# Transposing attention probabilities as float32r from tiles that a DMA fills

## The chip, the cores and the metric

The kernel runs on one core of a Trainium2 chip. The metric is the device time of one execution in microseconds. Below, PE is the matrix engine (TensorE), PEld its weight loads, DVE the vector engine, ACT the scalar engine, POOL the GpSimd engine, SP the engine that only issues DMAs.

## The reference

An encoder trunk of two layers on 512 tokens of width 1024. Layer 0 mixes tokens by gated linear attention, layer 1 by softmax attention, and each is followed by a gated MLP with a width-3 convolution. The change is in layer 1:

```python
def attn_mixer(h, w_qkv, q_norm, k_norm, w_out, cos, sin):
    ...                                  # q: 8 heads, k and v: 2, of 128; rmsnorm and rope on q and k
    scale = ATTN_HEAD_DIM ** -0.5
    def block(q_blk):                    # 128 queries of each head
        s = jnp.einsum('bkgqd,bksd->bkgqs', q_blk, k).astype(jnp.float32) * scale
        p = jax.nn.softmax(s, axis=-1).astype(v.dtype)
        return jnp.einsum('bkgqs,bksd->bkgqd', p, v)
    o = lax.map(block, qb)
    ...
    return o @ w_out
```

All of it is in float32.

## The kernel before

The activations `x` lie in SBUF as eight tiles of 128 features by 512 tokens. Nearly all matmuls are in float32r, a shorter form of float32: each operand is split into a high part, which is its float32r value, and a low part, the rest, and a product is three matmuls, high x high, high x low and low x high (`mm3`, lines 266 to 268; `out_steps`, line 323; `token_steps`, line 297). Weights arrive in tiles `raw` of 1 MB by SP's DMAs. `Weights.half` hands out one half after the other and makes the next one ready: either ACT and DVE split it (lines 143, 144), or, for the attention's query, key and value weights and part of the output's, ACT writes the high part and its negative and a DMA on POOL's queue adds `raw` to that (lines 123, 124, 133).

Attention runs over 32 blocks, 8 heads of 4 blocks with 128 queries each. For block t of the loop over `t`:

- `scores` (line 772): one `mm3` into a bank of the PSUM tag `s` (2 banks), then on DVE the row maximum `mx` (line 781) and the bias `nb` (782), then on ACT the exponential `p` (784), which also gives the row sums. A `p` is a float32 tile of 128 x 512 of the SBUF tag `t`, of which there are 6.
- `shares`: DVE inverts the sum (`rc`, 789) and scales `p` (790).
- `turn`: for the block LAG = 4 steps earlier, four transposes of 128 x 128 on PE into a bank of the tag `pt` (802), then ACT writes the high part `pth` (805) and DVE the low part `ptl` (806).
- `mix`: LAG2 = 6 steps behind, for every second block, twelve matmuls with the values into `po`.

Between them stand steps of other work, listed by `plan`: the projections of the query pairs 1 to 3 (`qpair`; `feature_steps` is the matmuls `A` and `B`, 48 instructions to a pair), placed by `Q_STEPS`, and what makes a pair ready (norm, rotation, splitting), placed by `Q_READY`. Each entry gives a first block and how many steps of the generator are taken at that block and the following ones. `O_STEPS` places twelve steps of the output projection `op`; the rest of it follows the loop. The recording layer that builds the program takes the order of the code as a priority and may move an instruction ahead of others; the order on each engine is fixed when the program is built.

A transpose of a float32 tile uses `ident`, a float32 identity. The same identity serves the linear attention (lines 489, 561) and the spreading of norms (line 207). The tag `sq` has 3 tiles: squares of `x` for the norms (lines 240, 244), squares of queries, and the router weights `rraw` of layer 0. The sums of squares go to PE as `ms` (line 252).

Of the kernel before, what the change touches and what calls it, by code (L numbers as in the profile page):

```python
# [8 lines left out]
F32 = mybir.dt.float32  # L9
F32R = mybir.dt.float32r  # L10
# [4 lines left out]
P = 128  # L15
S = 512
D = 1024
KC = D // P
# [10 lines left out]

GATE_STEPS, GATE_LAG = (1, 3, 5, 7, 10, 12, 15, 17), 2  # L30

LAGS = (4, 6)

Q_STEPS = {1: (0, (4,) * 4), 2: (4, (3, 3, 2, 2, 2, 2, 2)), 3: (11, (2,) * 8)}
Q_READY = {1: (4, (3, 3, 2, 1, 1, 0, 1)), 2: (11, (3, 2, 2, 1, 1, 1, 0, 1)), 3: (19, (3, 2, 2, 1, 1, 1, 0, 1))}

O_STEPS = (22, 23, 25, 27, 29, 31, 32, 33, 34, 35, 36, 37)


PC_NORM = 0  # L40
# [6 lines left out]
def hybrid_encoder_kernel(  # L47
# [20 lines left out]
    nc = tc.nc  # L68
    pe, act, dve, pool, sync = nc.tensor, nc.scalar, nc.vector, nc.gpsimd, nc.sync
    mm = pe.matmul  # L70

    cp = ctx.enter_context(tc.tile_pool(name="cp", bufs=1))
    sp = ctx.enter_context(tc.tile_pool(name="sp", bufs=1))
# [4 lines left out]
    def nm(s):  # L78
        uid[0] += 1
        return f"{s}{uid[0]}"  # L80
# [3 lines left out]
    def bank(tag, n):  # L84
        return pp.tile([P, S], F32, tag=tag, bufs=PS[tag], name=nm(n))
# [4 lines left out]
    def big(dt, n):  # L90
        return pair("g", 22, dt, n)

    def tmp(tag, n, w=S):
        return sp.tile([P, w], F32, tag=tag, bufs={"u": 4, "t": 6, "sq": 3}[tag], name=nm(n))

    def tiny(w, n, tag="tiny"):
        return sp.tile([P, 8], F32, tag=tag, bufs={"tiny": 36, "tiny2": 4}[tag], name=nm(n))[:, :w]
# [73 lines left out]
        sync.dma_start(raw[c // 4][:, r], w_vg[c // 4, :, r])  # L171
        W.raw[id(w_vg), c // 4] = raw[c // 4]

    ident = cp.tile([P, P], F32, name="ident")
    make_identity(nc, ident)

    two = tmp("u", "two")
    dve.memset(two[:, :P], 2.0 ** -5)
    dve.memset(two[:, P : 2 * P], -(2.0 ** -6))
# [30 lines left out]
    class Norm:  # L210
# [27 lines left out]
        def square(self, c):  # L238
            q = tmp("sq", "sq")
            act.activation(q, x[c], AF.Square)  # L240
            if self.ss is None:
                self.ss = q
            else:
                dve.tensor_tensor(self.ss, self.ss, q, ALU.add)
            self.done += 1
# [18 lines left out]
    def mm3(ps, wh, wl, mh, ml, start, stop):  # L264

        mm(ps, wh, mh, start=start, stop=False)  # L266
        mm(ps, wh, ml, start=False, stop=False)  # L267
        mm(ps, wl, mh, start=False, stop=stop)  # L268
# [74 lines left out]
    def gla(norm, nxt):  # L343
# [36 lines left out]
        cw = cp.tile([P, 2 * 2 * FC * 4], F32, name="cw")  # L380


        rraw = sp.tile([P, KC * 32], F32, tag="sq", bufs=3, name="rraw")
        sync.dma_start(rraw, w_r)
        rw = pair("wh", 3, F32R, "rw")
        rv = rraw.rearrange("p (k o c) -> p k o c", k=KC, o=1)
# [13 lines left out]
        norm.rows()  # L400

        rf = tmp("t", "rf")
        dve.tensor_tensor(rf, rp, norm.R, ALU.mult)
        rst = sp.tile([P, S], F32R, tag="t", bufs=6, name="rst")
        act.activation(rst, rf, AF.Copy)
        dve.tensor_tensor(rst[32:64, :], rf[32:64, :], rst[32:64, :].bitcast(F32), ALU.subtract)

# [228 lines left out]
    def attention(norm, nxt):  # L636
# [90 lines left out]
        def qpair(i, tag="acc"):  # L727
            head, sc = yield from roped(1 + i, PC_QK, float(HD), "qsc", tag)
            for e in range(2):
                y = head(e)  # L730
                yield
                t = big(F32R, "q")
                split(y, t)
                heads[2 * i + e] = (t, sc, e)
                yield
# [34 lines left out]
        probs, pts, pos = {}, {}, {}  # L770

        def scores(h, j):

            qt, sc, e = heads[h]
            kt = kk[h // 4]
            js = slice(j * P, (j + 1) * P)
            s = bank("s", "s")
            mm3(s, qt[:, js], qt[:, S + j * P : S + (j + 1) * P], kt[:, :S], kt[:, S:], True, True)
            scj = sc[:, 2 * j + e : 2 * j + e + 1]
            mx, nb, sm, rc = (tiny(1, n) for n in ("mx", "nb", "sm", "rc"))  # L780
            dve.reduce_max(mx, s, axis=mybir.AxisListType.X)
            dve.tensor_scalar(nb, mx, scj, -1.0, ALU.mult, ALU.mult)
            p = tmp("t", "p")
            act.activation(p, s, AF.Exp, scale=scj, bias=nb, accum_out=sm)
            probs[h, j] = (p, sm, rc)

        def shares(h, j):
            p, sm, rc = probs[h, j]
            dve.reciprocal(rc, sm)
            dve.tensor_scalar(p, p, rc, None, ALU.mult)  # L790
            probs[h, j] = p

        def turn(h, j):

            hf, i = divmod(j, 2)
            if i == 0:
                pts[h, hf] = tuple(big(F32R, n).rearrange("p (k q) -> p k q", q=256) for n in ("pth", "ptl"))
            ph3, pl3 = pts[h, hf]
            p = probs.pop((h, j))
            tp = bank("pt", "pt")  # L800
            for k in range(NT):
                pe.transpose(tp[:, k * P : (k + 1) * P], p[:, k * P : (k + 1) * P], ident)  # L802
            isl = slice(i * P, (i + 1) * P)
            tp3 = tp.rearrange("p (k q) -> p k q", q=P)
            act.activation(ph3[:, :, isl], tp3, AF.Copy)
            dve.tensor_tensor(pl3[:, :, isl], tp3, ph3[:, :, isl].bitcast(F32), ALU.subtract)

        def mix(h, hf):
            ph3, pl3 = pts.pop((h, hf))
            vo = (h // 4) * HD  # L810
            if hf == 0:
                pos[h] = bank("po", "po")
            dst = pos[h][:, hf * 256 : (hf + 1) * 256]
            for k in range(NT):
                vsl = slice(k * 256 + vo, k * 256 + vo + HD)
                mm3(dst, vh[:, vsl], vl[:, vsl], ph3[:, k, :], pl3[:, k, :], k == 0, k == NT - 1)
            if hf == 1:
                t = big(F32R, "oT") if h < 4 else pair("xhl", 8, F32R, "oT")
                split(pos[h], t)
                oh[h] = (t[:, :S], t[:, S:])  # L820

        LAG, LAG2 = LAGS
        blocks = [(h, j) for h in range(QH) for j in range(NT)]
        osteps = out_steps(w_aout, oh, nxt)
        plan = collections.defaultdict(list)
        for i in range(1, QH // 2):
            g = qpair(i)
            for first, counts in (Q_STEPS[i], Q_READY[i]):
                for t, n in enumerate(counts):
                    plan[first + t] += [g] * n  # L830
        for t in O_STEPS:
            plan[t].append(osteps)
        for t in range(len(blocks) + LAG2):
            if t < len(blocks):
                scores(*blocks[t])
            for g in plan[t]:
                next(g, None)
            if LAG <= t < len(blocks) + LAG:
                turn(*blocks[t - LAG])
            if t < len(blocks):  # L840
                shares(*blocks[t])
            if t >= LAG2:
                h, j = blocks[t - LAG2]
                if j % 2 == 1:
                    mix(h, j // 2)
        whole(osteps)

    norms = [Norm(i) for i in range(4)]
    cw = gla(norms[0], norms[1])
    ffn(0, norms[1], cw, norms[2])  # L850
    attention(norms[2], norms[3])
    ffn(1, norms[3], cw, None)

# [80 lines left out]
```

## Time and profile before

| | us |
|---|---|
| median of 3 runs (lowest, highest) | 1133.26 (1132.57, 1133.51) |
| the profiled execution, its own time | 1133.16 |
| its span | 1131.4 |
| PE busy, share of the span | 99% |
| DVE, ACT, POOL busy | 61%, 43%, 7% |
| first scores to last transposes of the attention | 625.4 to 734.2 |

The granted clock of PE is 1.00 over the run. A row of the profile names the line of the kernel, the engine, the operation, the tile that is written and those that are read. Matmuls overlap in their records, so their durations add up to more than their time; what one costs is the distance between the starts of two in a row. In the chain of work that ended last each step is followed back to what released it.

### The profile page before, as it was taken

Reading aid. Unit: us, or ns where it says so; the run is one execution under the profiler, and the core shown is the slowest. Engines: PE = TensorE matmul, PEld = TensorE weight load, DVE = VectorE, ACT = ScalarE, POOL = GpSimd, SP = SyncE. Lnnn points to the kernel's source line nnn. Section 1 sums busy time; section 2 is a strip of 40 time slices with the busy share of each in tenths; the row PEclk is TensorE's granted clock in tenths of the full one; section 3 lists DMA queues with packets and bytes.
Section 4 is the critical chain, followed back from the end, with each engine's and each line's share of the span. In section 5 each row is a group of like instructions: output and inputs, shape, how many; then the busy total and the mean of one; then the engine's idle time right before and its main releaser. Section 6 shows DMA issues by size and latency. Waiting matters only on the chain.

```text
span 1131.4 us, 12991 instructions
## 1 busy us (share of the span) xinstructions
PE 1125.7 (99%) x5260; PEld 939.2 (83%) x5260; DVE 690.1 (61%) x996; ACT 482.1 (43%) x690; POOL 76.0 (7%) x66
## 2 busy tenths in 40 slices
PE   9999999999999999999999999999999999999998
PEld 7888888888888888888888888888888888888887
DVE  6787563677777777633325589766777777762221
ACT  5564232444444444422234667644444444442210
POOL 0104110000000000000004433000000000000000
PEclk9999999999999999999999999999999999999999
DMA  6422211232322323223247633223232232323320
GB/s 231 149 75 78 84 63 38 75 112 75 112 97 90 112 75 112 100 86 112 77 152 181 149 76 75 56 75 112 75 112 85 101 112 75 112 84 121 130 93 19
DMA packets 19980, 111.66 MB, mean 99 GB/s; under 512 B 2384, under 2 KB 3024, under 8 KB 8400
## 3 DMA queue, kind: packets, MB, share of 16 engines
q1 hardware_dynamic: 17328, 102.29, 25.9%
q0 software_dynamic: 2304, 8.39, 3.9%
q8 instruction: 41, 0.67, 0.2%
q10 hardware_dynamic: 288, 0.15, 0.0%
q14 instruction: 19, 0.16, 0.0%
HBM read 100.34 MB, written 2.10 MB: 91 GB/s over the span
## 4 chain that ended last, share of the span: by engine, by line
PE 99%; DVE 0%; DMA 0%; ACT 0%; issue 0%; SPq 0%; DVEq 0%; ACTq 0%
PE up L266 14%; PE up L267 14%; PE up L268 14%; PE vg L297 8%; PE op L323 8%; PE dn L266 7%; PE dn L268 7%; PE dn L267 7%; PE o L548 2%; PE pt L802 1%; PE av L297 1%; PE kv L524 1%; PE A L266 1%; PE A L268 1%; PE A L267 1%; PE B L266 1%
## 5 line engine op out<-in xcount | busy, mean ns | idle before, releaser
L143 ACT ACTIVATE wh<-raw 128x1024 fp32r<-128x1024 f32 x164 | 173.3, 1056 | 351.4 <-PE up L267 132.8
L144 DVE TENSOR_TENSOR wl<-raw,wh 128x1024 fp32r<-128x1024 f32 x164 | 203.7, 1242 | 144.8 <-ACT wh L143 144.6
L266 PE MATMUL up<-xhl,wh 128*128 128x512 f32 x704 | 274.3, 390 | 0.0
L268 PE MATMUL up<-xhl,wl 128*128 128x512 f32 x704 | 273.9, 389 | 0.0
L267 PE MATMUL up<-xhl,wh 128*128 128x512 f32 x704 | 273.9, 389 | 0.0
L268 PEld LDWEIGHTS up<-xhl,wl 128*128 128x128 f32 x704 | 132.2, 188 | 27.6
L266 PEld LDWEIGHTS up<-xhl,wh 128*128 128x128 f32 x704 | 132.2, 188 | 27.4
L267 PEld LDWEIGHTS up<-xhl,wh 128*128 128x128 f32 x704 | 132.2, 188 | 27.1
L266 PE MATMUL dn<-gu,wh 128*128 128x512 f32 x352 | 136.9, 389 | 0.0
L267 PE MATMUL dn<-gu,wh 128*128 128x512 f32 x352 | 136.9, 389 | 0.0
L268 PE MATMUL dn<-gu,wl 128*128 128x512 f32 x352 | 136.9, 389 | 0.0
L603 DVE TENSOR_TENSOR u<-up,R 128x512 f32<-128x512 f32 x88 | 60.3, 687 | 52.7 <-PE up L268 52.7
L297 PE MATMUL vg<-wh,xhl 128*128 128x512 f32 x256 | 79.7, 390 | 0.6 <-DVE halfneg L184 0.6
L605 ACT ACTIVATE y<-u,cw 128x512 f32<-128x512 f32 x88 | 71.2, 811 | 20.4 <-DVE u L603 20.4
L268 PEld LDWEIGHTS dn<-gu,wl 128*128 128x128 f32 x352 | 66.1, 188 | 13.8
L267 PEld LDWEIGHTS dn<-gu,wh 128*128 128x128 f32 x352 | 66.1, 188 | 13.7
L266 PEld LDWEIGHTS dn<-gu,wh 128*128 128x128 f32 x352 | 66.1, 188 | 13.6
L323 PE MATMUL op<-oT,wh 128*128 128x512 f32 x256 | 70.9, 395 | 0.0
L607 DVE SCALAR_TENSOR_TENSOR y<-u,cw,y 128x511 f32<-128x511 f32 x88 | 65.9, 751 | 2.9
L606 DVE SCALAR_TENSOR_TENSOR y<-u,cw,y 128x511 f32<-128x511 f32 x88 | 65.6, 746 | 0.6 <-ACT y L605 0.6
L609 ACT ACTIVATE y<-y 128x512 f32<-128x512 f32 x44 | 27.9, 634 | 87.8 <-DVE y L607 87.8
L297 PEld LDWEIGHTS vg<-wh,xhl 128*128 128x128 f32 x256 | 48.0, 188 | 10.6 <-ACT sq L240 0.7
(186 smaller groups left out, 1432.1 us busy)
## 6 DMA issues: line engine op xcount, KB each, us to landing
raw<-in_w_up_dram SPq DMA_DIRECT2D x44, 1024.0 KB, 4.8
raw<-in_w_down_dram SPq DMA_DIRECT2D x22, 1024.0 KB, 4.8
wl<-raw POOLq DMA_DIRECT2D x16, 512.0 KB, 4.7
raw<-in_w_vg_dram SPq DMA_DIRECT2D x6, 1024.0 KB, 4.7
raw<-in_w_akq_dram SPq DMA_DIRECT2D x5, 1024.0 KB, 5.2
raw<-in_w_kq_dram SPq DMA_DIRECT2D x4, 1024.0 KB, 4.8
raw<-in_w_gout_dram SPq DMA_DIRECT2D x4, 1024.0 KB, 4.8
raw<-in_w_aout_dram SPq DMA_DIRECT2D x4, 1024.0 KB, 4.9
```

The lines of the kernel that those rows point to most:

```text
L143: act.activation(hi[:, sl], r[:, sl], AF.Copy)
L144: dve.tensor_tensor(lo[:, sl], r[:, sl], hi[:, sl].bitcast(F32), ALU.subtract)
L266: mm(ps, wh, mh, start=start, stop=False)
L267: mm(ps, wh, ml, start=False, stop=False)
L268: mm(ps, wl, mh, start=False, stop=stop)
L297: mm(ps[j][:, :width], hl[k][i == 2][:, j * P : (j + 1) * P], (wl if i == 1 else wh)[:, sl], start=k == 0 and i == 0, stop=k == KC - 1 and ...
L323: mm(pss[ng][n], wt[:, sl], mv, start=k == 0 and i == 0, stop=k == KC - 1 and i == 2)
L603: dve.tensor_tensor(u, ps, norm.R, ALU.mult)
L605: act.activation(y, u, AF.Identity, scale=w(1), bias=w(3))
L606: dve.scalar_tensor_tensor(y[:, 1:], u[:, : S - 1], w(0), y[:, 1:], ALU.mult, ALU.add)
L607: dve.scalar_tensor_tensor(y[:, : S - 1], u[:, 1:], w(2), y[:, : S - 1], ALU.mult, ALU.add)
L609: act.activation(res[1], res[1], AF.Silu)
```

## The change

Probabilities are no longer transposed from the tile in which they were computed. One block later a DMA on ACT's queue copies them, bit for bit, into a tile declared float32r, and the transposes read that tile, with an identity declared float32r. The loop turns a block five steps after its scores and mixes it seven steps after. Probabilities and copies share the tag `t`, now of seven tiles; the squares get two tiles instead of three, the router weights move from the squares' tag to `t`, and the identity is first made in a temporary tile and then copied. The pairs' projections and their making ready are placed anew (pair 1 in three blocks instead of four, pairs 2 and 3 evenly in eight, all made ready in seven blocks, so that each pair is complete one block sooner), and so are the steps of the output projection. In the built order PE's instructions outside the attention are the same as before. In the changed kernel the copies are line 800, the transposes line 812, their evacuation lines 815 and 816, the scaling line 794 and the exponential line 788.

```diff
-LAGS = (4, 6)
-
-Q_STEPS = {1: (0, (4,) * 4), 2: (4, (3, 3, 2, 2, 2, 2, 2)), 3: (11, (2,) * 8)}
-Q_READY = {1: (4, (3, 3, 2, 1, 1, 0, 1)), 2: (11, (3, 2, 2, 1, 1, 1, 0, 1)), 3: (19, (3, 2, 2, 1, 1, 1, 0, 1))}
-
-O_STEPS = (22, 23, 25, 27, 29, 31, 32, 33, 34, 35, 36, 37)
+LAGS = (5, 7)
+
+Q_STEPS = {1: (0, (5, 5, 6)), 2: (3, (2,) * 8), 3: (11, (2,) * 8)}
+Q_READY = {i: (t, (3, 3, 2, 1, 1, 0, 1)) for i, t in ((1, 3), (2, 11), (3, 19))}
+
+O_STEPS = (22, 24, 26, 28, 30, 32, 33, 34, 35, 36, 37, 38)
...
-        return sp.tile([P, w], F32, tag=tag, bufs={"u": 4, "t": 6, "sq": 3}[tag], name=nm(n))
+        return sp.tile([P, w], F32, tag=tag, bufs={"u": 4, "t": 7, "sq": 2}[tag], name=nm(n))
...
-    ident = cp.tile([P, P], F32, name="ident")
-    make_identity(nc, ident)
+
+    eye = tmp("u", "eye")[:, :P]
+    make_identity(nc, eye)
+    identr = cp.tile([P, P], F32R, name="ident")
+    dve.tensor_copy(identr, eye)
+    ident = identr.bitcast(F32)
...
-        rraw = sp.tile([P, KC * 32], F32, tag="sq", bufs=3, name="rraw")
+        rraw = sp.tile([P, KC * 32], F32, tag="t", bufs=7, name="rraw")
...
-        rst = sp.tile([P, S], F32R, tag="t", bufs=6, name="rst")
+        rst = sp.tile([P, S], F32R, tag="t", bufs=7, name="rst")
...
+        def copy(h, j):
+
+            t = sp.tile([P, S], F32R, tag="t", bufs=7, name=nm("pr"))
+            act.dma_start(t.bitcast(F32), probs[h, j])
+            probs[h, j] = t
+
...
-                pe.transpose(tp[:, k * P : (k + 1) * P], p[:, k * P : (k + 1) * P], ident)
+                pe.transpose(tp[:, k * P : (k + 1) * P].bitcast(F32R), p[:, k * P : (k + 1) * P], identr)
...
         for t in range(len(blocks) + LAG2):
             if t < len(blocks):
                 scores(*blocks[t])
+            if 1 <= t <= len(blocks):
+                copy(*blocks[t - 1])
```

## The prediction

> **What bounds the kernel now.** I read the page first, for the engine that carries the span, then the transposes by their tile, then the neighbours of the same shape for what a faster transpose could cost, and last the waits and the timeline where the attention's engines meet.
>
> ```profile
> PE 1125.7 (99%) x5260; PEld 939.2 (83%) x5260; DVE 690.1 (61%) x996; ACT 482.1 (43%) x690; POOL 76.0 (7%) x66
> PE 99%; DVE 0%; DMA 0%; ACT 0%; issue 0%; SPq 0%; DVEq 0%; ACTq 0%
> ```
>
> The first line is busy time, the second the shares of the chain that ended last. TensorE (PE) is on that chain for 99% of the span of 1131.4 us. So time goes or comes only as PE time: a matmul that becomes shorter, or a gap that opens in PE's row. Nothing outside the attention changes PE's instructions; there the 128 transposes of the probabilities are what the change makes shorter.
>
> ```profile
> L802 PEld LDWEIGHTS pt<-ident,p x128: 137/139/227, 643.6 to 734.1; 128*128 128x128 f32 x128
> L802 PE MATMUL pt<-ident,p x128: 270/272/309, 643.8 to 734.2; 128*128 128x128 f32 x128
> ...
> 649.57 0.60 PE L802 MATMUL pt<-ident,p 128*128 128x128 f32 x4
> ...
> 121.96 1.95 PE L501 MATMUL in<-ek 128*128 128x128 f32 x16
> 234.21 0.95 PE L252 MATMUL ms<-ones,sq 128*128 128x1 f32 x8
> ...
> L501 PEld LDWEIGHTS in<-ek x64: 190/192/192, 121.8 to 175.7; 128*128 128x128 f32 x64
> L501 PE MATMUL in<-ek x64: 275/275/275, 122.0 to 175.8; 128*128 128x128 f32 x64
> ...
> L252 PE MATMUL ms<-ones,sq x32: 164/250/250, 27.3 to 773.3; 128*128 128x1 f32 x32
> ...
> 614.09 11.52 PE av L297 x96
> ...
> 740.11 27.23 PE op L323 x120
> ```
>
> Matmuls overlap in their records, so what one costs is its pace, start to start. Four transposes last 0.60 us and one 0.272, so the pace is (0.60 - 0.272) / 3 = 0.109 us, and 128 of them are 14.0 us of PE. The last two rows are pieces of the chain, of float32r matmuls only: 256 columns (av) at 11.52 / 96 = 0.120 us, 512 columns (op) at 27.23 / 120 = 0.227 us. That is 0.107 us for 256 columns more, and 0.013 us that each matmul costs beside its columns. The plain float32 matmuls "in" have 128 columns and yet a pace of (1.95 - 0.275) / 15 = 0.112 us.
>
> **The change, part by part.** *The transposes.* The same 128 instructions, now with float32r data and identity. If a float32r transpose streams its 128 columns once, the row of float32r matmuls gives 0.013 + 0.107 / 2 = 0.067 us. It then saves 0.109 - 0.067 = 0.042 us, times 128 = 5.4 us. Two things bound this. The weight load must keep up: an ordinary load ("in") is recorded at 192 ns and holds a pace of 0.100 to 0.112 us ("ms" has a single column to stream, so there is nothing but the load: (0.95 - 0.25) / 7 = 0.100); that of a transpose is 139 ns, 53 less, which leaves 0.047 to 0.059, under 0.067. If the 0.013 is not paid, the pace is that load's at most 0.059 and the saving 6.4 us. At the other end, with the load of an ordinary float32r matmul, nothing is saved (the first rival). I take 5.4, because the row for the load of a transpose is the nearest one.
>
> *The copies.* 32 DMAs of 256 KB, from SBUF to SBUF, issued on ACT's queue, each behind the exponential of the next block. The trace has no such DMA; the nearest are the stores of the output, of the same size, and the one that ACT issues at the end.
>
> ```profile
> out_dram<-x SPq DMA_DIRECT2D x7, 256.0 KB, 2.1
> ...
> 1128.61 0.36 ACTq L633 DMA_DIRECT2D out_dram<-x  x1
> ...
> DMA to landing us min/median/max: 1.7/2.0/4.6
> ...
> 630.00:645.00 15.00, 15.00 (x73) 12.32 (x73) 9.91 (x24) 9.67 (x17) 3.46 (x4) 1.00 0.83 200
> 690.00:705.00 15.00, 14.74 (x98) 12.75 (x97) 13.24 (x31) 10.68 (x22) 7.87 (x6) 1.00 0.19 36
> ```
>
> A copy holds ACT's sequencer for 0.36 us. What is queued behind it on ACT is the evacuation of the transposed block and then the next exponential. The window rows give PE, PEld, DVE, ACT and POOL busy: ACT, at its fullest, is busy 10.68 of 15 us, with 15 / 2.74 = 5.5 blocks in them (the step between the two exponentials quoted below); 5.5 x 0.36 = 2.0 us more still fits. At best the issue runs while the exponential before it executes (0.78 us) and costs nothing. A copy waits for the scaled probabilities; in DVE's queue these stand ahead of the next block's bias, for which the exponential ahead of the copy waits anyway, so ACT's queue gets no new wait from them. Copies are landed by the store row in 2.1 us, between 1.7 and 4.6.
>
> Whether this shows on PE is a matter of the distance from scaling to transpose. In the built order of the changed kernel the early transposes stand five blocks behind; in the last third they stand directly behind the scores of three or four blocks later, as they do now:
>
> ```profile
> 715.30 0.48 DVE L790 TENSOR_SCALAR p<-p,rc 128x512 f32<-128x512 f32 x1
> 717.97 0.48 DVE L790 TENSOR_SCALAR p<-p,rc 128x512 f32<-128x512 f32 x1
> ...
> 716.40 0.78 ACT L784 ACTIVATE p<-s,nb,qsc 128x512 f32<-128x512 f32 x1
> 719.14 0.77 ACT L784 ACTIVATE p<-s,nb,qsc 128x512 f32<-128x512 f32 x1
> ...
> 719.88 0.27 PE L802 MATMUL pt<-ident,p 128*128 128x128 f32 x1
> 721.66 0.60 PE L802 MATMUL pt<-ident,p 128*128 128x128 f32 x4
> ...
> PEld s L266 <- ACT p L784: 1.7, 4, 0.7
> PE s L266 <- ACT p L784: 0.3, 1, 0.3
> ```
>
> These are blocks 26 and 27: scaled by 715.78 and 718.45, transposed from 719.88 and 721.66. A copy issued at the next block's exponential (716.40, 719.14) and landed 2.1 us later is there at 718.5 and 721.24: 1.4 and 0.4 us ahead of the transpose. So at 2.1 us it is hidden, with little to spare. The bounds are 0 and the second rival's 8.4 us; I take 1.0 us, for the half of a dozen late blocks where 0.4 us or less is left. The last two rows are the waits that exist now, where scores wait for a bank that an exponential still reads: at most 2.0 us, and I leave them as they are, since PE's work per block in that third stays at about the 2.74 us between the exponentials (the op groups that moved make up for the shorter transposes). If they went, that would be 2.0 us more of gain.
>
> *Seven tiles.* Probabilities and copies share them. In the built order nearly every exponential waits for the landing of a copy issued two blocks earlier, over 5 us; one or two copies wait for the one issued a block earlier, about 3 us. Hidden at 2.1, and at 4.6 part of the second rival.
>
> *Pairs a block sooner.* The projection's matmuls are the same in number. The third pair's weights are needed sooner by one group of scores, 3 matmuls at op's 0.227 = 0.7 us of PE, while the first copies share the DMA engines (0.83 busy in the window row above).
>
> ```profile
> raw<-in_w_up_dram SPq DMA_DIRECT2D x44, 1024.0 KB, 4.8
> ...
> 629.57 0.89 POOL L133 DMA_DIRECT2D wl<-raw  x1
> 641.16 0.39 PE L268 MATMUL A<-xhl,wl 128*128 128x512 f32 x1
> DMA to landing us min/median/max: 5.0/5.4/9.1
> ```
>
> The load issued at 629.57 is the one of 9.1 us: landed by 638.7, used at 641.16, 2.5 us later. 0.7 less leaves 1.8; a copy ahead of it takes some quarter of a 1024 KB load's 4.8 us, 1.2 us. One is hidden, two cost 0.6. I put it at nothing, and the 0.6 into the range.
>
> *Two square buffers instead of three, the identity, the router's tile.* The square of the last chunk now waits for the addition of the one before.
>
> ```profile
> 769.68 0.62 ACT L240 ACTIVATE sq<-x 128x512 f32<-128x512 f32 x1
> ...
> 770.14 0.68 DVE L244 TENSOR_TENSOR sq<-sq,sq 128x512 f32<-128x512 f32 x1
> 771.41 0.68 DVE L244 TENSOR_TENSOR sq<-sq,sq 128x512 f32<-128x512 f32 x1
> 772.61 0.95 PE L252 MATMUL ms<-ones,sq 128*128 128x1 f32 x8
> ```
>
> 770.82 + 0.62 (a square) + 0.68 = 772.12 instead of 772.09, and PE asks at 772.61. The extra copy of the identity is a DVE instruction of under 1 us ahead of the first transposes. Nothing.
>
> *Sum.* The profiled execution took 1133.16 us (span 1131.4 and 1.8 around it); the median of the runs is 1133.26. 1133.2 - 5.4 + 1.0 = 1128.8 us.
>
> **The rivals.** *First: the transposes are no faster.* Either float32r still streams two passes (0.109 as now), or its weight load is the ordinary one and holds 0.100 to 0.112 us. For it speaks that both the "in" row and the transposes stand near 0.11 with 128 columns, against it that the load of a transpose is recorded shorter. It saves between 1.2 and -0.4 us; with the 1.0 for the copies 1133.0 to 1134.6, about 1133.8. The Trainium skill, "TensorE: Matmul & The Clock Gate", section "LDWEIGHTS (loading the stationary operand)", has the rule that speaks for this rival: a load takes its columns / 1.2 in ns, 107 for 128 columns, as an estimate from that page; the "in" row agrees with it. By that rule the saving would be 0.3 us. The same page, section "Terms", calls the transpose mode four times faster for FP32, which would point the other way; the 0.109 of the transposes against twice 0.112 for a plain float32 matmul (two rows each) shows a factor of two so far.
>
> *Second, and slower: the copies become PE's wait.* The mechanism is one loop: scores, exponential, copy, transpose, and behind the transpose in PE's queue the scores of a block some three further on. If a copy lands in 4.6 us, the store's maximum, block 27 above is 2.1 us late, and since the loop spans three blocks, the last 12 pay it four times: 8.4 us. 1133.2 - 5.4 + 8.4 = 1136.2. It begins to cost at a landing of 2.5 us and eats the whole saving at 2.1 + 0.4 + 5.4 / 4 = 3.9 us. For it speaks how little is left at block 27, against it that DMA is 0.19 busy there. The Trainium skill, "DMA: Bandwidth & Descriptors", section "Anatomy of one DMA", gives 2.0 us and bytes / 436e3 for a DMA from GpSimd's queue, 2.6 for 256 KB as an estimate from that page; the store row, at 2.1, is shorter.
>
> *Third: all of it hidden, the faster load.* 6.4 saved and no wait: 1126.8; with the present waits gone 1124.8.
>
> **How the numbers follow.** No change is within 0.2%, 2.3 us, which is about what a measurement of this kernel can tell: 1131.0 to 1135.5. Forecast and third rival together 0.59 (the third 0.12 of it), range 1126 to 1131. First rival 0.19, mostly within 2.3 us, a third of it with more than 1 us for the copies and then slower. Second 0.22: with landings between 2.5 and 4.6 its times run from 1129 to 1137 and, where the exponentials wait too, to 1140; 0.01 faster, 0.05 no change, 0.16 slower. That gives 0.60 faster, 0.17 the same, 0.23 slower. The likeliest is 1128.8. From 1126.0 to 1137.5 some 0.07 lie below and some 0.1 above.
>
> **What would show it.** Right: the transposes' group at a pace near 0.067 us and their loads still near 139 ns; copies landed in 2 to 2.5 us; waits of PE for a DMA under 1 us in all. The first rival shows as loads of 188 to 192 ns or matmuls still at 272 and a pace of 0.10 or more. The second shows as idle PE ahead of transposes, put down to the copy's DMA, after about 690 us. The prediction is wrong if scores wait for exponentials by over 4 us in all, or if a stage outside the attention has become longer.

## The result, and the profile after

| | before | after |
|---|---|---|
| median of 20 runs each on one chip (lowest, highest), us | 1133.28 (1132.57, 1133.88) | 1134.86 (1133.58, 1136.44) |
| ratio of the times, 95% interval | | 1.0014 (1.0007 to 1.0020) |
| the profiled execution, its own time, us | 1133.16 | 1135.43 |
| its span, us | 1131.4 | 1133.7 |

The change costs 1.6 us (0.8 to 2.3) where 4.4 us less were forecast. The first rows are from the page of the changed kernel: busy times, and the copies among the DMA issues.

```profile
PE 1124.7 (99%) x5260; PEld 938.0 (83%) x5260; DVE 690.4 (61%) x997; ACT 482.2 (43%) x690; POOL 75.8 (7%) x66
...
pr<-p ACTq DMA_DIRECT2D x32, 256.0 KB, 2.6
```

PE is busy 1.0 us less and yet the span is 2.3 us longer: PE waits more. Now the transposes and copies by their tile.

```profile
L812 PEld LDWEIGHTS pt<-ident,pr x128: 137/140/224, 646.9 to 736.4; 128*128 128x128 f32 x128
L812 PE MATMUL pt<-ident,pr x128: 221/244/282, 647.1 to 736.5; 128*128 128x128 f32 x128
L800 ACTq DMA_DIRECT2D pr<-p x32: 472/472/527, 632.9 to 731.5; - x32
...
DMA to landing us min/median/max: 2.2/2.6/7.4
```

The loads are as they were (140 ns against 139), the matmuls' records 28 ns shorter. A copy is issued in 0.47 us and lands after 2.6 us in the median, but after up to 7.4. What four transposes cost is read from PE's timeline, where scores follow them. The first three rows are the kernel before, the last three the one after.

```profile
656.01 0.60 PE L802 MATMUL pt<-ident,p 128*128 128x128 f32 x4
656.37 0.48 PE L266 MATMUL s<-k,q 128*128 128x512 f32 x1
656.68 0.40 PE L267 MATMUL s<-k,q 128*128 128x512 f32 x1
```

```profile
659.81 0.46 PE L812 MATMUL pt<-ident,pr 128*128 128x128 f32 x4
660.10 0.47 PE L270 MATMUL s<-k,q 128*128 128x512 f32 x1
660.41 0.39 PE L271 MATMUL s<-k,q 128*128 128x512 f32 x1
```

From the first transpose to the second matmul of the scores there were 0.67 us, and there are now 0.60; the other groups of a block give the same difference, 0.07, in the median. One of the scores' matmuls takes 0.23 in a row of its own kind, so four transposes cost 0.44 us before and 0.37 after: 0.109 and 0.092 us each. 32 blocks save 32 x 0.07 = 2.2 us.

The other part is the waits, here those of PE and of the exponential from 640 to 740 us (in total, times, longest):

```profile
PE s L270 <- ACT p L788: 2.0, 2, 1.3
...
ACT p L788 <- DMA pr<-p: 1.7, 1, 1.7
...
PE pt L812 <- DMA pr<-p: 1.5, 1, 1.5
```

Three places hold most of it. They are read from the timeline of ACT, that of PE, and the chain of waits:

```profile
645.38 0.47 ACTq L800 DMA_DIRECT2D pr<-p  x1
...
652.84 0.78 ACT L788 ACTIVATE p<-s,nb,qsc 128x512 f32<-128x512 f32 x1 [1.68 <-DMA pr<-p]
652.89 0.47 ACTq L800 DMA_DIRECT2D pr<-p  x1
```

```profile
653.76 0.50 PE L270 MATMUL s<-k,q 128*128 128x512 f32 x1 [1.28 <-ACT p L788]
...
722.78 0.25 PE L812 MATMUL pt<-ident,pr 128*128 128x128 f32 x1 [1.48 <-DMA pr<-p]
```

```profile
699.43 1.37 POOL ry L699
700.83 0.64 ACT q L705
...
717.80 4.84 DMA pr<-p
722.78 0.25 PE pt L812
```

The exponential of block 6 stands until 652.84, when a copy issued at 645.38 has landed, 7.4 us after its issue, since it takes that copy's tile; the next copy (652.89) stands behind it in ACT's queue. Two blocks on, PE's scores (653.76) wait for the bank that this exponential reads: PE starts them 1.5 us later than its usual distance from the transposes ahead of them. At 722.78 the transposes of block 26 wait for a copy that took 4.84 us, and PE loses 1.6 us in the same count. A third, 0.9 us at 702.3, goes through POOL's rotation of the last pair and ACT's queue, not straight through a landing.

### The profile page after: what moved, and what is told of

It reads as the page before. It is cut to its first block, busy times and chain, and to the rows that moved or that the text cites. A ratio compares the mean times of both kernels' runs of the same rounds, so it can differ in the third digit from the quotient of the medians.

```text
span 1133.7 us, 13083 instructions
## 1 busy us (share of the span) xinstructions
PE 1124.7 (99%) x5260; PEld 938.0 (83%) x5260; DVE 690.4 (61%) x997; ACT 482.2 (43%) x690; POOL 75.8 (7%) x66
```

## The experiments

Theory 1: a float32r transpose saves 0.07 us a block, not 0.17. Theory 2: the copies' landings cost PE some 3.5 us, 2a through the seven tiles (an exponential waits for a landing), 2b through transposes that wait for a late copy. Theory 3: the moved steps cost this, with or without copies. Each run was timed against the kernel before on its own chip.

| kernel | us, median | against before, us | ratio, 95% interval |
|---|---|---|---|
| after | 1134.86 | +1.6 | 1.0007 to 1.0020 |
| before, float32r transposes, no copies | 1131.07 | -2.2 | 0.9971 to 0.9989 |
| after, no copies, float32r | 1131.38 | -1.9 | 0.9974 to 0.9992 |
| after, no copies, float32 | 1133.45 | +0.2 | 0.9994 to 1.0011 |
| after, copies, float32 | 1135.64 | +2.4 | 1.0009 to 1.0027 |
| after, eighth tile | 1132.59 | -0.9 | 0.9985 to 1.0003 |
| after, copy ahead of the scores | 1134.86 | +1.4 | 1.0003 to 1.0020 |
| after, last eight blocks plain | 1133.59 | +0.1 | 0.9992 to 1.0010 |
| after, eighth tile and last eight plain | 1131.36 | -2.1 | 0.9972 to 0.9990 |
| after, w_aout's low parts by VectorE | 1137.01 | +3.7 | 1.0018 to 1.0044 |
| after, eighth tile and low parts by VectorE | 1134.82 | +1.5 | 1.0005 to 1.0023 |
| after, four blocks behind | 1134.31 | +1.0 | 1.0004 to 1.0021 |
| after, four behind and last eight plain | 1131.87 | -1.4 | 0.9978 to 0.9996 |

**The parts of the change taken apart: four kernels.**

```diff
 # 1: the kernel before, with the identity made as in the kernel after, the scaling reading p as float32, and
-            p = tmp("t", "p")
+            p = sp.tile([P, S], F32R, tag="t", bufs=6, name=nm("p"))
-                pe.transpose(tp[:, k * P : (k + 1) * P], p[:, k * P : (k + 1) * P], ident)
+                pe.transpose(tp[:, k * P : (k + 1) * P].bitcast(F32R), p[:, k * P : (k + 1) * P], identr)
 # 2: the kernel after, with the same tile for p (7 of them), and
-            if 1 <= t <= len(blocks):
-                copy(*blocks[t - 1])
 # 3: the kernel after without these two lines, and
-                pe.transpose(tp[:, k * P : (k + 1) * P].bitcast(F32R), p[:, k * P : (k + 1) * P], identr)
+                pe.transpose(tp[:, k * P : (k + 1) * P], p[:, k * P : (k + 1) * P], ident)
 # 4: the kernel after with its copies, and
-                pe.transpose(tp[:, k * P : (k + 1) * P].bitcast(F32R), p[:, k * P : (k + 1) * P], identr)
+                pe.transpose(tp[:, k * P : (k + 1) * P], p[:, k * P : (k + 1) * P].bitcast(F32), ident)
```

> The kernel before with its schedule, but the probabilities' tiles are float32r, written so by the exponential and the multiplication by the reciprocal, and transposed as float32r; no copies. Left out: the bits of the probabilities that float32r doesn't hold. It prices the transposes alone. Prediction's step (pace 0.067 us instead of 0.109): 5.4 us faster than before, 1127.9. Theory 1 (first of a block 0.06, the other three held by their weight loads at 0.083, and 0.07 more before the next matmul, 0.056 saved in a block): 1.8 us faster, about 1131.5; with the head's 0.55 of after, if that comes from the float32r identity, 1132.0.

> The changed kernel without the copies: its schedule and lags, its seven tiles, its head, and float32r transposes read from tiles that the exponential and the multiplication write as float32r. Left out: the bits that float32r doesn't hold. Theory 2 (the copies' landings cost PE about 3.5 to 4 us of waits in the attention): about 3.5 faster than after, 1131 to 1131.5. Theory 3 (the moved steps and lags cost these waits, copies or not): as after, 1134.5 to 1135.

> The changed kernel without the copies and with float32 transposes from the exponentials' tiles, as before the change: what is left is the schedule, the lags, the seven tiles and the head. Theory 2: as before, plus at most the 0.55 of the head, 1133.0 to 1134.0. Theory 3: 3.5 above before, about 1136.5. Prediction (moved steps cost nothing): 1133.2.

> The changed kernel with its copies, but the four transposes of a block in float32 from the copied tile. Theories 1 and 2: the 1.8 of the transposes comes back, 1136 to 1136.7, or less where the longer transposes hide a wait. Prediction's step: 5.4 above after, about 1140. Theory that transposes are no faster at all: as after, 1134.9.

The transposes alone give 2.2 us in the schedule of before (first kernel) and 1133.45 - 1131.38 = 2.1 in that of after (second against third). That is theory 1 and not 5.4. Schedule, lags, seven tiles, two square tiles and the identity together give +0.2, with an interval of -0.7 to 1.2: theory 3 falls. The copies cost 1134.86 - 1131.38 = 3.5 us with float32r and 1135.64 - 1133.45 = 2.2 with float32 transposes. There PE waits 2.5 us for exponentials and not at all for a copy; that the longer transposes hide the rest is likely, but not shown. The terms add up, as differences of the same four times must: -2.1 + 3.5 + 0.2 = +1.6. Two of the four kernels, with float32r and no copies, leave out the bits of the probabilities that float32r doesn't hold, so they price the parts and are no substitutes. Without copies the waits of PE for the exponential and for a DMA are gone; these are all waits of PE that the view lists for the second kernel in the attention:

```profile
PE op L327 <- DVE oT L706: 0.3, 1, 0.3
PE pt L812 <- DVE ptl L816: 0.3, 1, 0.3
```

**Which wait of the copies: four kernels.**

```diff
 # 5: an eighth tile
-            p = tmp("t", "p")
+            p = sp.tile([P, S], F32, tag="R", bufs=1, name=nm("p")) if (4 * h + j) % 3 == 2 else tmp("t", "p")
 # 6: the copy ahead of the scores
+            if 1 <= t <= len(blocks):
+                copy(*blocks[t - 1])
             if t < len(blocks):
                 scores(*blocks[t])
-            if 1 <= t <= len(blocks):
-                copy(*blocks[t - 1])
 # 7: the last eight blocks plain (N_COPY = 24; turn transposes a float32 tile with ident)
-            if 1 <= t <= len(blocks):
+            if 1 <= t <= N_COPY:
 # 8: 5 and 7 together
```

> The changed kernel with an eighth tile for the probabilities: the exponential of every third block writes into the tile R, which nothing uses during the attention. Theory 2a (an exponential has to wait for the landing of an earlier copy because only seven tiles are there, and through it PE at two places, 1.5 us and 0.95 us): about 2.4 faster than after, 1132.4. Theory 2b (what costs is that the last blocks' transposes wait for late copies, and traffic): at most 0.3 faster, 1134.5 to 1134.9. Prediction's step (the seven tiles hide it): as after.

> The changed kernel with one statement moved: the copy of block t-1 is issued ahead of the scores and the exponential of block t, not behind them. In ACT's queue a copy then no longer stands behind an exponential that itself waits for the copy before. Theory 2a with the queue's order as cause (copy, landing, exponential, next copy follow one another at 2.5 to 4.5 us a block, as long as PE's work for a block): 2 to 2.5 faster than after, 1132.4 to 1132.9. Rival: ACT now waits for DVE's multiplication ahead of every exponential, and later exponentials hold PE: 1 or more slower than after, 1136 and above. Prediction's step (a copy adds no wait in ACT's queue): as after, 1134.9.

> The changed kernel, but the last eight blocks (24 to 31) aren't copied: they are transposed in float32 from the exponentials' tiles. Theory 2b: the wait of 1.65 us ahead of block 26's transposes and part of the smaller ones behind it go, the eight blocks' transposes cost 8 times 0.056 = 0.45 more, so 1.2 to 1.7 faster than after, 1133.2 to 1133.7. Theory 2a alone (early waits are made up for nowhere, late ones would follow from them): 0.5 slower to 0.5 faster than after.

> Both of the two before: the eighth tile, and the last eight blocks plain. If 2a and 2b are separate and between them hold the copies' whole cost: the time without copies, 1131.4, plus 0.45 for eight plain blocks, 1131.8, and so faster than before with all bits kept. If the copies cost also by their traffic or by ACT's time for the issues: 1132.5 to 1133.5.

PE's waits for an exponential and for a copy, in this order for the kernels 5 to 8:

```profile
PE pt L812 <- DMA pr<-p: 1.2, 1, 1.2
PE s L270 <- ACT p L788: 0.4, 1, 0.4
```

```profile
PE pt L812 <- DMA pr<-p: 3.3, 2, 2.2
```

```profile
PE s L272 <- ACT p L790: 1.9, 2, 1.2
```

```profile
PE s L272 <- ACT p L790: 0.4, 1, 0.4
```

The fifth and the seventh edit each take away (to 0.4 us) their own row and leave the other. The eighth tile gains 2.5 us (from +1.6 to -0.9), plain late blocks gain 1.5, both together 3.7, and with both the time is that without copies: 1131.36. (Eight float32 blocks should cost it 8 x 0.07 = 0.6 more; the intervals, some 1 us either way, don't resolve that.) So tile reuse and late transposes hold the copies' whole cost, and neither the 0.47 us that each of the 24 copies left takes of ACT's queue nor their traffic costs anything that could be measured beside them. One limit: in the traces the eighth tile also changes the order of some PE instructions, from 665 us on, and plain late blocks do so from 715 on. That the 0.9 us at 702.3 was the tile's and not the order's isn't shown. The 1.5 us at 653.76 is: the order up to there is the same, and the exponential's row names the copy. For the 1.6 at 722.78 the row of the changed kernel names the copy, but with plain late blocks PE's steps ahead of it have moved too.

The sixth kernel refutes that the queue's order alone is to blame. The exponentials no longer wait for copies (no such row is left), but two blocks of transposes now wait 3.3 us for theirs, and the median is as after (the profiled execution, 1133.39, was the fastest of eleven). The chain only hands its wait on, to whoever needs a late copy next.

The eighth kernel copies the probabilities bit for bit, or transposes them in float32, and is 0.10 to 0.28% faster than before; it is the fastest of those that round nothing to fill a float32r tile.

**Why a copy lands late: four kernels.** In the changed kernel a copy takes 2.3 us where nothing large is in flight and up to 7.4 where something is. The copies by their tile from 700 to 714 us, then from 714 to 729, and last the accumulating DMA `wl`, issued at 715.9:

```profile
L800 ACTq DMA_DIRECT2D pr<-p x5: 472/472/472, 700.9 to 712.4; - x5
DMA to landing us min/median/max: 2.2/2.3/2.3
```

```profile
L800 ACTq DMA_DIRECT2D pr<-p x5: 472/472/472, 715.5 to 726.9; - x5
DMA to landing us min/median/max: 2.4/2.9/4.8
```

```profile
L133 POOL DMA_DIRECT2D wl<-raw x1: 917/917/917, 715.9 to 715.9; - x1
DMA to landing us min/median/max: 6.1/6.1/6.1
```

The copy issued at 717.80 landed at 722.64, 0.6 us after that DMA (issued at 715.86, landed at 722.00).

```diff
 # 9: fewer accumulating DMAs
-    W.by_dma += [(a, 1) for a in qk_order + [w_av]] + [(w_aout, 2)]
+    W.by_dma += [(a, 1) for a in qk_order + [w_av]] + [(w_aout, 1)]
 # 10: 9 with the eighth tile
 # 11: transposes four blocks behind; 12: 11 with the last eight blocks plain
-LAGS = (5, 7)
+LAGS = (4, 7)
```

> The changed kernel, but the low parts of the second block of w_aout (two halves of 512 KB) are made by VectorE's subtraction, not by the accumulating DMAs that run during blocks 18 to 26. Theory 2b (copy 26 lands 4.84 us after its issue because an accumulating DMA is in flight, where a copy alone lands in 2.3): copy 26 lands in under 3.5 us and PE's wait of 1.65 us ahead of its transposes goes, 1.0 to 1.7 faster than after, 1133.2 to 1133.9, the early waits stay. Rival (a copy lands late by itself or by ACT's order): copy 26 lands as late as before, time as after or later by the subtractions, 1134.9 to 1135.5.

> The eighth tile and the low parts by VectorE together, all 32 blocks copied. If 2a and 2b hold the copies' whole cost: 2.4 + 1.4 below after, 1131.0 to 1131.5, some 0.4 below what eight plain blocks gave if nothing else is late. If other late copies (28, beside the last load of w_aout) hold PE too: 1131.5 to 1132.5.

> The changed kernel with transposes four blocks behind instead of five: each copied tile comes free a block sooner, so that with the same seven tiles an exponential reuses the tile of the block three before it and not of two before it. Theory 2a: the early waits (1.5 and 0.95 us) go without an eighth tile, 1.5 to 2.5 faster than after, 1132.4 to 1133.4, unless the transposes, now a block closer to their copies, take these waits over (a landing of 7.4 us against three blocks of 2.5 to 4 us): then as after or up to 1.5 slower, 1134.9 to 1136.4.

> Four blocks behind, and the last eight blocks plain. Theories 2a and 2b: 1131.5 to 1132.0, as with the eighth tile; if the transposes take over the early waits: 1133 to 1134.5.

The ninth kernel's median is 2.1 us above the changed kernel's, outside what was expected either way. Its copies and its load of `w_aout` from 714 to 729 us:

```profile
L800 ACTq DMA_DIRECT2D pr<-p x5: 472/472/472, 714.8 to 728.4; - x5
  DMA pr<-p: 2.1, 1
DMA to landing us min/median/max: 2.3/4.1/7.0
```

```profile
L118 SPq DMA_DIRECT2D raw<-in_w_aout_dram x1: 327/327/327, 715.8 to 715.8; - x1
DMA to landing us min/median/max: 8.2/8.2/8.2
```

Without the accumulating DMA, which reads `raw`, that tile was free sooner, and the 1 MB load that used to be issued at 722.12 was issued at 715.83. Copy 26, issued at 717.70, landed at 724.69, 0.7 us after that load (landed at 724.03). One large transfer went and another took its place; the copy waited for it in the same way, and longer. In the changed kernel and in this one a copy that meets no large transfer lands in 2.2 to 2.5 us throughout (10 and 14 copies). So the reading that a copy lands behind whatever large transfer is in flight stands, on two different transfers; the edit as a remedy fails. (It also moves some of PE's steps, from 693 us on.) Its 2.1 us above after are something else, seen in the windows of this kernel (us of the stretch, busy time and count of PE, PEld, DVE, ACT, POOL, then the granted clock, DMA share and GB/s):

```profile
720.00:725.30 5.30, 1.94 (x11) 1.19 (x10) 2.56 (x6) 1.84 (x4) 0.00 (x0) 0.83 0.31 119
725.30:729.30 4.00, 4.00 (x11) 3.03 (x11) 1.98 (x6) 2.22 (x5) 0.00 (x0) 0.50 0.17 66
729.30:735.00 5.70, 5.70 (x38) 5.10 (x36) 3.28 (x8) 2.06 (x4) 0.00 (x0) 0.91 0.36 138
```

Behind two waits of PE, 1.3 and 2.1 us long, the granted clock is 0.50 for 4 us. That execution took 1139.07, and its granted clock over the whole span is 0.997. Since 4 us at half the clock lower that figure by 0.002, it tells which of the others had such a stretch: three of the seven have 1.000 and took 1134.91 to 1135.32, four have 0.996 to 0.998 and took 1137.01 to 1140.25. So at the full clock the ninth kernel takes about what the changed kernel takes, 1134.86, and what its median has above that goes with the half clock. That is also the time expected for a copy late by itself or by ACT's order; against this speak the copies that met no large transfer. The tenth kernel shows the half clock behind one wait of 2.7 us for a late copy (0.55 for 2.8 us, so 1.3 us more), and all its eleven executions have 0.998; the two together are enough for its missing the expected 1131 to 1132.5.

Four blocks behind (eleventh) gains only 0.5 of the 1.5 to 2.5 expected: no exponential waits for a copy, but transposes do, with PE idle for 0.4 us at 650.31, 0.4 at 719.08 and 1.3 at 726.76, each 0.1 us behind the landing of their copy (two of these rows name a DVE instruction instead), as the second half of the expectation had it. With the last eight blocks plain it comes to 1131.87, within the 1131.5 to 1132.0 of theories 2a and 2b.

## Why the prediction was wrong, step by step

*PE bounds the kernel; outside the attention nothing changes.* Right. In the profiled execution the first scores start 0.55 us later than before (626.00 against 625.45), but in two kernels with the same head they start 0.10 sooner and 0.01 later, so this is from run to run. Behind the attention the distance stays as it is.

*The transposes, 5.4 us.* This is the first term that was mis-sized: 2.1 to 2.2 us measured. The step that failed is "the weight load must keep up". The prediction took the 53 ns by which the record of a transpose's load is shorter off the pace of an ordinary load, had 0.047 to 0.059 us, and let the 0.067 of the columns decide. The record stayed at 140 ns, but the pace isn't what that subtraction gives. These are the last three loads of the block shown above and the next one behind them, first before, then after:

```profile
656.02 0.36 PEld L802 LDWEIGHTS pt<-ident,p 128*128 128x128 f32 x3
656.34 0.19 PEld L266 LDWEIGHTS s<-k,q 128*128 128x128 f32 x1
```

```profile
659.81 0.31 PEld L812 LDWEIGHTS pt<-ident,pr 128*128 128x128 f32 x3
660.07 0.19 PEld L270 LDWEIGHTS s<-k,q 128*128 128x128 f32 x1
```

Loads started 0.11 us apart and now start (660.07 - 659.81) / 3 = 0.087 apart, not under 0.067. The first transposes of a group follow closer ((0.46 - 0.244) / 3 = 0.072 us in the mean), but up to the second matmul behind the group each costs 0.092. Whether the loads hold the transposes or the transposes the loads was not tested by itself. The Trainium skill, "TensorE: Matmul & The Clock Gate", section "Back-to-back issue gap", gives some 81 ns for each pair of a load and a matmul of 128 columns in a sustained stream; by that, as an estimate from that page, 128 x (0.109 - 0.081) = 3.6 us would be saved. The 0.087 between loads is close to it; the measured 2.2 is less, but nearer to it than the forecast was.

*The copies, 1.0 us.* The second term, 3.5 us. The landing came as forecast only where nothing else was in flight: 2.3 us against 2.1 from the row of the stores. The step that failed is taking the median of that row for the attention. The row itself held the warning: its maximum, 4.6 us, is a store beside a 1 MB load. In the kernel before, the two are issued thus, and the load lands after 5.3 us, the store after 4.6:

```profile
1037.47 0.33 SPq L118 DMA_DIRECT2D raw<-in_w_down_dram  x1
1038.79 0.34 SPq L629 DMA_DIRECT2D out_dram<-x  x1
```

```profile
DMA to landing us min/median/max: 5.3/5.3/5.3
```

```profile
DMA to landing us min/median/max: 4.6/4.6/4.6
```

So the store landed at 1043.4, 0.6 us behind the load (1042.8), just as copies do. A second store of the seven, issued at 1083.66 with a load in flight, took 3.1 us; the other five took 2.0 to 2.1. The attention is full of such transfers: the prediction's own window row has a DMA share of 0.83 from 630 to 645 us, and in the changed kernel the share, last but one in this row, is 0.65.

```profile
640.00:700.00 60.00, 58.72 (x356) 50.52 (x355) 49.86 (x114) 40.77 (x76) 23.23 (x19) 1.00 0.65 184
```

The 2.6 us that the prediction estimated from the Trainium skill, "DMA: Bandwidth & Descriptors", section "Anatomy of one DMA", are for a DMA from GpSimd's queue; that the median here is 2.6 as well bears little, since it lies between copies alone, at 2.2 to 2.5, and late ones. The issue took 0.47 us, not 0.36, and cost nothing that shows.

*"ACT's queue gets no new wait", and the seven tiles "hidden".* Both wrong, and one mechanism: an exponential waits for the landing of the copy whose tile it takes, and the next copy stands behind it. The prediction saw the wait, and priced it as a distance of over 5 us against a landing of 2.1; the landing was 7.4. It even named 4.6 as the end where it costs, for the late blocks alone, and argued against that with a DMA share of 0.19, read from 690 to 705 us. The wait came at block 6, where large transfers are in flight.

*Existing waits left as they are.* They did not stay: PE's own row was 0.3 us, is 2.0 in the changed kernel, and 0.4 with the eighth tile.

*Pairs a block sooner, two square tiles, identity, router's tile: nothing.* Right: +0.2 in all, within the interval.

*The rivals.* The second named the right place and the right row, PE ahead of transposes behind the copy's DMA after 690 us. Its price was wrong, 8.4 us for four turns of a loop. The wait came once, for 1.5 us, because copies that meet no large transfer land in 2.3 us and the loop recovers. The first rival came out in part: the saving lies between its 1.2 and the forecast's 5.4. The time, 1134.86, is 6.1 us above the likeliest and on the other side of the time before. That a bit of each happened is the sum of two errors, not something the prediction foresaw.

## What to carry to other kernels

A small DMA on which an engine's next instruction depends must be priced beside the large transfers of its own stretch, not by a median from a quiet one: look up what was in flight at the slowest instance of the row. Where it may land late, give its tile a successor or leave the most urgent pieces out of it. An instruction that becomes shorter inside a short group is priced by the distance across the whole group to the second instruction behind it, and the rest of the saving looked for there. Taking one transfer away can bring the next one forward into the same place.

## What the runs showed of the hardware

- A copy of 256 KB inside SBUF lands in 2.2 to 2.5 us where no large transfer is in flight (ten copies of the changed kernel). In that kernel and the ninth, each copy issued while a 512 KB or 1 MB transfer on another queue was in flight landed behind it, in some half of the cases by 0.2 to 0.7 us, and up to 7.4 us after its own issue. There are other causes: two copies of the tenth kernel, issued at 652.35 and 653.10, took 4.1 and 4.0 us though the last large transfer had landed.
- In the profiled executions PE ran at about half its clock for 2.8 us behind a wait of 2.7 us, and for 4 us behind two of 1.3 and 2.1 close together. Behind 2.2 us in the sixth kernel it did not, but four of that kernel's eleven executions have a clock of 0.998. PE's timeline of the ninth kernel:

```profile
727.60 0.63 PE L270 MATMUL s<-k,q 128*128 128x512 f32 x1
728.03 0.63 PE L271 MATMUL s<-k,q 128*128 128x512 f32 x1
728.46 0.63 PE L272 MATMUL s<-k,q 128*128 128x512 f32 x1
```

  0.43 us for 512 columns, where it is 0.23 otherwise; 4 us at half the clock make 2.0 us. The Trainium skill, "TensorE: Matmul & The Clock Gate", section "Wait — 56ns, not 53.3ns?", gives 426.7 ns for 512 columns on a cold array; these rows agree. So these waits of PE cost themselves and 1.3 to 2.0 us more. The time does not always show it: six of the eleventh kernel's eleven executions have 0.998, and the fastest is one of them. The spread of the changed kernel's runs, 2.9 us, is not this: none of them is under 0.999, and the two slowest have 1.000. What spreads them stays open.
